# A four-layer hybrid decoder step on one core: the last S5 layer's parameter products are formed in the feed-forward before it and kept in DRAM

## The chip, the cores and the metric

The kernel runs on one core of a Trainium2 chip. The core has TensorE (matmul), VectorE, ScalarE and GpSimd, and a SyncE queue (SP) from which DMAs are issued. The metric is device time of one execution in microseconds; the median of several runs counts. The stretches of time below are microseconds from the start of the profiled span.

## The reference

One inference step of a four-layer trunk, for 512 prompt positions and 8 single-token samples that share all weights (width 1024, all in float32). Layer 0 and layer 3 have an S5 mixer, layer 1 stick-breaking attention, layer 2 a chunked gMLP; each mixer is followed by a SwiGLU feed-forward of width 2816, and every sub-layer stands between two RMS norms. The S5 mixer, shortened:

```python
u  = xn @ w_in                                   # 64 groups of 16 channels
ar, ai = mag * cos(li * dt), mag * sin(li * dt)  # one complex decay per group and state
bur = einsum('blgp,gnp->lbgn', ug, b_re)         # inputs to 64 states per group
...
hr, hi = scan(h[l] = a * h[l-1] + q * bu[l])     # complex, over the positions
y = einsum('lbgn,gpn->blgp', hr, c_re) - einsum('lbgn,gpn->blgp', hi, c_im) + d_skip * u
out = val * sigmoid(gate),  val, gate = split(gelu(y) @ w_glu)
```

The products that the change moves hold parameters alone: powers of the decay a times B (input matrix), C times powers of a (output matrix), and C a^k B (chunk matrix). None of them depends on x.

## The kernel before

Activations lie transposed: 8 tiles of 128 channels by 520 columns (512 positions, 8 samples), in two halves of 256 and 264. All weight products are done in three float32r matmuls (high times high, high times low, low times high; `mm`, L233 to L236). A weight tile of 128 output channels is loaded to `raw` (L194, two buffers), rounded to `wh` on ScalarE (L204) and its rest formed to `wl` on VectorE (L206). SP, ScalarE and VectorE do that some items ahead of TensorE.

A small planner writes the program. TensorE's work moves a model clock `self.t` on (`pe`); generators (`spawn`) run beside it and give, by `yield`, after how much model time, or on which condition, their next piece is put into the program. `until` runs the generators on till a condition holds. A scheduler then fixes each engine's order from that program with a timing model; on the chip each engine, and SP as a queue, works strictly in that order.

Between two sub-layers stands a *turn* (`turn`, L410 on): for each half the last output items end, the mean square is summed on TensorE, an inverse root made on VectorE and spread by a matmul (L365), then VectorE and ScalarE form the new x and its high and low parts (L421, L423, L405, L406), and the same sum, root and spread (a second L365) give the scale `rs` of the next sub-layer.

The S5 layer cuts 512 positions into 64 chunks of 8. `s5_begin` and `s5_prep` make the small tables (decays' powers `ap`, `b`, `c`); for the last layer that is done beside the gMLP. `s5_pipe` then goes over 8 tiles of 128 channels. Per tile it forms

- `powers_b` (L735 to L737): `ba` = B times powers, six products of 512 elements, on GpSimd (VectorE for tile 0), with `tn` as scratch;
- `powers_c` (L751, L761 to L763): `ca` = C times powers, half on VectorE, half on GpSimd, with `at` a copy of the powers and `tm` scratch;
- `blocks` and `kernels` (L743, L771, L776, L777): the chunk matrix from `ca` and `bd` on TensorE, written to DRAM as `dk` and read back shifted by eight DMAs as `wn` (L784);
- `inputs`: `rot` loaded (L789), `ba` transposed on TensorE (L797) and copied to `wi` (L800);
- `chunks`: the tile's `u` stored to DRAM and read back by chunk as `uq` (L805, L808);
- `scan`: matmuls with `wi` (L819), rotation, running scan and rotation back on VectorE (L827 to L843);
- `outputs` and `finish`: matmuls of `uq` with `wn` and `hm` with `ca` (L851, L852), transposes (L864), gelu.

The pipeline runs as a generator; `u` of the tiles comes from the layer's input matmuls, the first four in both halves first. When all eight outputs are there, the GLU follows. In the feed-forward (`ffn`) 22 hidden tiles are made in chunks of 6, 8 and 8 (`CHUNKS`), each followed by a pass over the 8 output tiles. In the feed-forward before the last S5 layer, TensorE has these matmuls and nothing else.

## Time and profile before

| | us |
|---|---|
| runs, median of 3 | 2790.7 (2788.12 to 2790.83) |
| the profiled execution's own time | 2778.86 |
| its span | 2777.1 |
| TensorE busy | 2552.3 (92%) |
| VectorE busy | 1592.4 (57%) |
| ScalarE busy | 1020.6 (37%) |
| GpSimd busy | 567.5 (20%) |

The span is read by stage: the feed-forward of layer 2 lies from about 1675 to 2080, the turn from it to the S5 layer from 2068 to 2131, the tile pipeline of the S5 layer from there to 2271, then GLU, and the last feed-forward. A stretch in which TensorE is busy throughout is limited by it; where it is not, the chain of waits and the other engines' busy time say by what.

### The profile page before, as it was taken

Reading aid. Unit: us, or ns where it says so; the run is one execution under the profiler, and the core shown is the slowest. Engines: PE = TensorE matmul, PEld = TensorE weight load, DVE = VectorE, ACT = ScalarE, POOL = GpSimd, SP = SyncE. Lnnn points to the kernel's source line nnn. Section 1 sums busy time; section 2 is a strip of 40 time slices with the busy share of each in tenths; the row PEclk is TensorE's granted clock in tenths of the full one; section 3 lists DMA queues with packets and bytes.
Section 4 is the critical chain, followed back from the end, with each engine's and each line's share of the span. In section 5 each row is a group of like instructions: output and inputs, shape, how many; then the busy total and the mean of one; then the engine's idle time right before and its main releaser. Section 6 shows DMA issues by size and latency. Waiting matters only on the chain.

```text
span 2777.1 us, 49812 instructions
## 1 busy us (share of the span) xinstructions
PE 2552.3 (92%) x20826; PEld 2442.3 (88%) x20826; DVE 1592.4 (57%) x2702; ACT 1020.6 (37%) x1697; POOL 567.5 (20%) x564
## 2 busy tenths in 40 slices
PE   7769999999897888999999899999997679999998
PEld 5659999999885557999999899999997569999998
DVE  8883643434659985734346777343458864634344
ACT  5443433222345464432223654322233433432221
POOL 5661300000337841200001203000004730200000
PEclk8879999999999999999999999999998889999998
DMA  4533233332245753233324231333322524233331
GB/s 116 144 94 93 69 92 107 92 92 77 97 125 177 225 160 100 69 99 92 92 77 96 84 113 58 106 99 92 92 73 50 138 51 130 59 102 92 92 92 45
DMA packets 476544, 274.49 MB, mean 99 GB/s; under 512 B 51912, under 2 KB 458720, under 8 KB 476320
## 3 DMA queue, kind: packets, MB, share of 16 engines
q1 hardware_dynamic: 467104, 237.76, 30.4%
q0 software_dynamic: 9216, 33.56, 3.6%
q8 instruction: 164, 2.69, 0.4%
q14 instruction: 60, 0.49, 0.1%
HBM read 253.60 MB, written 17.66 MB: 98 GB/s over the span
## 4 chain that ended last, share of the span: by engine, by line
PE 48%; DVE 11%; ACT 3%; DMA 2%; issue 2%; POOL 1%; SPq 0%; ACTq 0%; DVEq 0%; POOLq 0%
PE pp L233 15%; PE pp L234 15%; PE pp L236 15%; DVE wl L206 1%; DVE m L1241 1%; DMA raw<-in_w_ffn_in_dram 1%; ACT wh L204 1%; DVE pn L421 1%; DVE x L423 1%; DVE hm L843 1%; DMA raw<-in_w_cm_out_dram 1%; POOL x L423 0%; DVE xl L406 0%; PE psr L365 0%; DVE o L831 0%
## 5 line engine op out<-in xcount | busy, mean ns | idle before, releaser
L233 PE MATMUL pp<-xh,wh 128*128 128x264 f32 (+1 forms) x4480 | 1205.3, 287 | 25.5 <-ACT xh L405 4.7
L234 PE MATMUL pp<-xl,wh 128*128 128x264 f32 (+1 forms) x4480 | 1208.6, 286 | 7.1 <-DVE xl L406 7.0
L236 PE MATMUL pp<-xh,wl 128*128 128x264 f32 (+1 forms) x4480 | 991.4, 285 | 7.3 <-POOL wl L206 5.6
L233 PEld LDWEIGHTS pp<-xh,wh 128*128 128x128 f32 x4480 | 851.0, 190 | 36.3 <-issue 6.5
L234 PEld LDWEIGHTS pp<-xl,wh 128*128 128x128 f32 x4480 | 853.0, 190 | 11.4 <-DVE xl L406 9.9
L204 ACT ACTIVATE wh<-raw 128x1024 fp32r<-128x1024 f32 (+1 forms) x376 | 390.2, 1041 | 1126.5 <-PE pp L234 808.1
L236 PEld LDWEIGHTS pp<-xh,wl 128*128 128x128 f32 x4480 | 737.0, 190 | 12.0 <-POOL wl L206 5.8
L206 DVE TENSOR_TENSOR wl<-raw,wh 128x1024 fp32r<-128x1024 f32 (+1 forms) x356 | 439.1, 1236 | 322.0 <-ACT wh L204 310.8
L234 PE MATMUL pp<-hl,wh 128*128 128x256 f32 (+1 forms) x1408 | 377.2, 283 | 0.0
L233 PE MATMUL pp<-hh,wh 128*128 128x256 f32 (+1 forms) x1408 | 376.0, 283 | 0.0
L236 PE MATMUL pp<-hh,wl 128*128 128x256 f32 (+1 forms) x1408 | 314.4, 282 | 0.0
L234 PEld LDWEIGHTS pp<-hl,wh 128*128 128x128 f32 x1408 | 265.1, 188 | 0.0
L233 PEld LDWEIGHTS pp<-hh,wh 128*128 128x128 f32 x1408 | 264.9, 188 | 0.0
L236 PEld LDWEIGHTS pp<-hh,wl 128*128 128x128 f32 x1408 | 231.4, 188 | 0.0
L1579 DVE TENSOR_TENSOR tg<-pp,rs 128x520 f32<-128x520 f32 (+2 forms) x100 | 62.6, 632 | 231.9 <-PE pp L236 231.9
L1590 DVE TENSOR_TENSOR tg<-pp,tg 128x520 f32<-128x520 f32 (+2 forms) x96 | 62.6, 653 | 221.5 <-PE pp L236 221.2
L338 POOL TENSOR_TENSOR acc<-acc,s 128x256 f32<-128x256 f32 (+1 forms) x96 | 83.6, 870 | 450.2 <-ACT s L334 447.8
L1602 DVE TENSOR_TENSOR op<-pp,op 128x520 f32<-128x520 f32 (+2 forms) x88 | 48.4, 550 | 178.9 <-PE pp L236 178.8
L206 POOL TENSOR_TENSOR wl<-raw,wh 128x1024 fp32r<-128x1024 f32 x20 | 48.4, 2424 | 332.7 <-ACT wh L204 314.8
L405 ACT ACTIVATE xh<-x,gt 128x264 fp32r<-128x264 f32 (+1 forms) x128 | 62.9, 505 | 59.0 <-DVE x L423 45.1
L406 DVE SCALAR_TENSOR_TENSOR xl<-x,gt,xh 128x264 fp32r<-128x264 f32 (+1 forms) x128 | 78.7, 631 | 1.6 <-ACT xh L405 1.2
L642 POOL MEMSET ap<- 128x32 f32 x2 | 0.3, 175 | 359.0 <-PE pp L236 359.0
(334 smaller groups left out, 2890.7 us busy)
## 6 DMA issues: line engine op xcount, KB each, us to landing
raw<-in_w_ffn_in_dram SPq DMA_DIRECT2D x176, 512.0 KB
raw<-in_w_ffn_out_dram SPq DMA_DIRECT2D x64, 512.0 KB
raw<-in_w_ssm_glu_dram SPq DMA_DIRECT2D x32, 512.0 KB
raw<-in_w_ffn_out_dram SPq DMA_DIRECT2D x32, 384.0 KB
raw<-in_w_sb_qkv_dram SPq DMA_DIRECT2D x24, 512.0 KB
raw<-in_w_ssm_in_dram SPq DMA_DIRECT2D x16, 512.0 KB
wn<-dk SPq DMA_DIRECT2D x128, 64.0 KB
raw<-in_w_cm_in_dram SPq DMA_DIRECT2D x16, 512.0 KB
```

The costliest lines, as they stand in the source:

```text
L204: nc.scalar.activation(wh[:, :nk], raw[:, :nk], AF.Copy)
L206: on.tensor_tensor(wl[:, :nk], raw[:, :nk], wh[:, :nk], op=ALU.subtract)
L233: nc.tensor.matmul(ps(*h), lhsT=wh[:, k, :], rhs=xh[:, h[0]:h[1]], start=first, stop=False)
L234: nc.tensor.matmul(ps(*h), lhsT=wh[:, k, :], rhs=xl[:, h[0]:h[1]], start=False, stop=False)
L236: nc.tensor.matmul(ps(*h), lhsT=wl[:, k, :], rhs=xh[:, h[0]:h[1]], start=False, stop=last)
L338: i = (nc.gpsimd if pool else nc.vector).tensor_tensor(acc[0][:, c0:c1], acc[0][:, c0:c1], sq[:, :n], op=ALU.add)
L405: nc.scalar.activation(xs[k][0][:, c0:c1], self.x[k][:, c0:c1], AF.Copy, scale=g)
L406: return nc.vector.scalar_tensor_tensor(xs[k][1][:, c0:c1], self.x[k][:, c0:c1], g, xs[k][0][:, c0:c1], op0=ALU.mult, op1=ALU.subtract)
L421: nc.vector.scalar_tensor_tensor(t[:, :n], ops[k][:, c0:c1], self.gain(which_post, layer, k), ps[:, :n], op0=ALU.mult, op1=ALU.mult)
L1579: v.tensor_tensor(g, ps(c0, c1), rs[:, c0:c1], op=ALU.mult)
L1590: v.tensor_tensor(t, ps(c0, c1), t, op=ALU.mult)
L1602: v.tensor_tensor(o, ps(c0, c1), o, op=ALU.add)
```

## The change

A new generator `s5_stash` runs beside the feed-forward of layer 2. It forms, for each of the 8 tiles, `ba` and its transpose `wi`, `ca`, and the chunk matrix (with all element-wise products on VectorE), and stores them to DRAM tiles `wid`, `cad` and `wnd`, the chunk matrix already shifted, by eight stores. In `s5_pipe`, where these are there (`kept`), `powers_b`, `powers_c`, `kernels` and `blocks` are left out, and `inputs` loads `wi`, `ca` and `wn` instead; `wi` and `rot` get two buffers. The feed-forward with a stash works in chunks of 4, 6, 6, 6, with 7 instead of 9 buffers for hidden tiles, and waits before its last output items until the stash is issued. In all feed-forwards the silu is done in place, without the tile `sg`. Layer 0's S5 is not changed.

```diff
--- before.py
+++ after.py
@@ -27,6 +27,7 @@
 DFF = 2816
 FT = DFF // 128
 CHUNKS = (6, 8, 8)
+CHUNKS2 = (4, 6, 6, 6)
 EPS = 1e-6
 MAGIC = 12582912.0
 LA = 2
@@ -52,6 +53,7 @@
 WX = (4, 4, 2, 4)
 GMY = (12.0, 6.0, 14.0, 0.5)
 OLA, FLA = 4, 2
+STASH = (5.0, 3.0)
 TWO_PI_DOWN = 6.283185
 
 
@@ -710,11 +712,83 @@
         S["ok"] = True
         p.release()
 
+    def s5_stash(self, j):
+
+        nc, v = self.nc, self.nc.vector
+        S = self.S5[j]
+        p = self.tc.alloc_tile_pool(name="s5w", bufs=1, side="right")
+        wi_d = S["wi"] = [self.dr.tile([128, 2, 512], F32, name=f"wid{t}", bufs=1) for t in range(KT)]
+        ca_d = S["ca"] = [self.dr.tile([128, 8, 144], F32, name=f"cad{t}", bufs=1) for t in range(KT)]
+        wn_d = S["wn"] = [self.dr.tile([128, 8, 128], F32, name=f"wnd{t}", bufs=1) for t in range(KT)]
+        bd = p.tile([128, 4, 2, 2, 16], F32, name="bdw")
+        nc.gpsimd.memset(bd, 0.0)
+        B, ap, C = S["b"], S["ap"], S["c"]
+        for t in range(KT):
+            P = slice(4 * t, 4 * t + 4)
+            at = p.tile([128, 2, 4, 2, 9], F32, tag="at", name="atw")
+            for d in range(2):
+                for b in range(2):
+                    s = slice(64 * b, 64 * b + 64)
+                    nc.scalar.activation(at[64 * d:64 * d + 64, :, :, b, :], ap[s, :, P, :], AF.Copy)
+                    nc.scalar.activation(bd[64 * d:64 * d + 64, :, b, b, :], B[s, d, P, :], AF.Copy)
+            for ri in range(2):
+                ba = p.tile([128, 4, 8, 16], F32, tag="ba", name="baw")
+                m1 = p.tile([128, 576], F32, tag="m1", name="m1w")
+                m = m1[:, :512].rearrange("p (a r c) -> p a r c", a=4, r=8)
+                bb = [B[:, q, P].unsqueeze(2).to_broadcast([128, 4, 8, 16]) for q in (ri, 1 - ri)]
+                ab = [ap[:, q, P, 7::-1].unsqueeze(3).to_broadcast([128, 4, 8, 16]) for q in range(2)]
+                v.tensor_tensor(ba, bb[0], ab[0], op=ALU.mult)
+                v.tensor_tensor(m, bb[1], ab[1], op=ALU.mult)
+                v.tensor_tensor(ba, ba, m, op=ALU.subtract if ri == 0 else ALU.add)
+                yield STASH[0]
+                ps = self.bk.tile([128, 512], F32, tag="b", name="psw")
+                for a in range(4):
+                    nc.tensor.transpose(ps[:, 128 * a:128 * a + 128], ba[:, a].rearrange("p r c -> p (r c)"), self.ident)
+                self.t += 0.45
+                wi = p.tile([128, 512], F32, tag="wi", name="wiw")
+                nc.scalar.activation(wi, ps, AF.Copy)
+                nc.sync.dma_start(wi_d[t][:, ri], wi)
+                yield STASH[1]
+            ps = None
+            for hf in range(2):
+                G = slice(8 * t + 4 * hf, 8 * t + 4 * hf + 4)
+                sh = [128, 4, 9, 16]
+                ca = p.tile([128, 4, 9, 16], F32, tag="ca", name="caw")
+                m = p.tile([128, 576], F32, tag="m1", name="m1w").rearrange("p (g k c) -> p g k c", g=4, k=9)
+                cs = [C[:, q, G].unsqueeze(2).to_broadcast(sh) for q in range(2)]
+                ad = [at[:, q].rearrange("p a b k -> p (a b) k")[:, 4 * hf:4 * hf + 4].unsqueeze(3).to_broadcast(sh)
+                      for q in range(2)]
+                v.tensor_tensor(ca, cs[0], ad[0], op=ALU.mult)
+                v.tensor_tensor(m, cs[1], ad[1], op=ALU.mult)
+                v.tensor_tensor(ca, ca, m, op=ALU.subtract)
+                nc.sync.dma_start(ca_d[t][:, 4 * hf:4 * hf + 4], ca.rearrange("p g k c -> p g (k c)"))
+                yield STASH[0]
+                if ps is None:
+                    ps = self.bk.tile([128, 512], F32, tag="b", name="pskw")
+                for g in range(2):
+                    for a in (2 * hf, 2 * hf + 1):
+                        nc.tensor.matmul(ps[32 * a:32 * a + 32, :128], lhsT=bd[:, a, g].rearrange("p g c -> p (g c)"),
+                                         rhs=ca[:, 2 * a + g - 4 * hf, 0:8].rearrange("p k c -> p (k c)"),
+                                         start=g == 0, stop=g == 1, tile_position=(0, 32 * a))
+                self.t += 0.3
+                if hf == 0:
+                    yield STASH[1]
+            kp = self.kpad[t % 2]
+            nc.scalar.activation(kp[:, 144:], ps[:, 16:128], AF.Copy)
+            v.scalar_tensor_tensor(kp[:, 128:144], self.mod, self.gt[:, 128 + j * KT + t:129 + j * KT + t], ps[:, :16],
+                                   op0=ALU.mult, op1=ALU.add)
+            for r in range(8):
+                nc.sync.dma_start(wn_d[t][16 * r:16 * r + 16].rearrange("p g x -> g p x"),
+                                  kp[:, 128 - 16 * r:256 - 16 * r])
+            yield STASH[1]
+        p.release()
+
     def s5_pipe(self, S, us, ready, pools, rot, j, zs):
 
         nc, v, gp = self.nc, self.nc.vector, self.nc.gpsimd
         T = [{} for _ in range(KT)]
         pa = pools["a"] = self.tc.alloc_tile_pool(name="s5a", bufs=1)
+        kept = "wi" in S
 
         def sl(t):
             return slice(4 * t, 4 * t + 4)
@@ -784,13 +858,21 @@
                 nc.sync.dma_start(wn[16 * r:16 * r + 16], dv[:, :, 128 - 16 * r:256 - 16 * r])
 
         def inputs(t):
-            ba = T[t]["ba"]
-            rot_ = T[t]["rot"] = tp.tile([128, 4, 2, 64], F32, tag="rot", name="rot", bufs=1)
+            rot_ = T[t]["rot"] = tp.tile([128, 4, 2, 64], F32, tag="rot", name="rot", bufs=1 + kept)
             nc.sync.dma_start(rot_, rot[:, sl(t)])
             rho = T[t]["rho"] = tp.tile([128, 4, 64], F32, tag="rho", name="rho", bufs=1)
             nc.scalar.activation(rho, S["rho"][:, sl(t)].unsqueeze(2).to_broadcast([128, 4, 64]), AF.Copy)
             gp.memset(rho[:, :, 0:1], 0.0)
+            if kept:
+                wi = T[t]["wi"] = tp.tile([128, 2, 4, 128], F32, tag="wi", name="wi")
+                nc.sync.dma_start(wi.rearrange("p i a c -> p i (a c)"), S["wi"][t])
+                ca = T[t]["ca"] = pa.tile([128, 8, 9, 16], F32, tag="ca", name="ca", bufs=3)
+                nc.sync.dma_start(ca.rearrange("p g k c -> p g (k c)"), S["ca"][t])
+                wn = T[t]["wn"] = tp.tile([128, 8, 128], F32, tag="wn", name="wn")
+                nc.sync.dma_start(wn, S["wn"][t])
+                return
             pt, _ = self.pair()
+            ba = T[t]["ba"]
             for ri in range(2):
                 for a in range(4):
                     q = 4 * ri + a
@@ -872,8 +954,9 @@
         def stage(f, t):
             if 0 <= t < KT:
                 f(t)
-        powers_b(0)
-        powers_c(0)
+        if not kept:
+            powers_b(0)
+            powers_c(0)
         yield lambda: S["ok"]
         tp = pools["t"] = self.tc.alloc_tile_pool(name="s5t", bufs=2)
         S["uq"] = [tp.tile([128, 8, 80], F32, name=f"uq{q}", bufs=1) for q in range(3)]
@@ -887,9 +970,9 @@
         for q in [h[:, :, :, 8] for h in S["hm"]] + [S["bd"]]:
             gp.memset(q, 0.0)
         for t in range(-3, KT + 1):
-            if t > -2:
+            if t > -2 and not kept:
                 stage(powers_b, t + 2)
-            if t > -1:
+            if t > -1 and not kept:
                 stage(powers_c, t + 1)
             if 0 <= t + 1 < KT:
                 if t < 0:
@@ -897,8 +980,9 @@
                 stage(scan, t + 1)
                 yield S5Y[1]
             stage(finish, t - 1)
-            stage(kernels, t + 1)
-            stage(blocks, t + 2)
+            if not kept:
+                stage(kernels, t + 1)
+                stage(blocks, t + 2)
             yield S5Y[2]
             stage(inputs, t + 2)
             yield S5Y[3]
@@ -1563,7 +1647,10 @@
         w_in, w_out = self.w["ffn_in", l], self.w["ffn_out", l]
         xs, rs = st["xs"], st["rs"]
         wide = nxt is not None and nxt[1] % 3 != 0
-        with tc.tile_pool(name="hp", bufs=9) as hp, tc.tile_pool(name="ft", bufs=2) as ft, \
+        stash = nxt is not None and not wide
+        chunks = CHUNKS2 if stash else CHUNKS
+        keep = self.spawn(self.s5_stash(nxt[1] // 3)) if stash else None
+        with tc.tile_pool(name="hp", bufs=max(chunks) + 1) as hp, tc.tile_pool(name="ft", bufs=2) as ft, \
                 tc.tile_pool(name="wx", bufs=WX[2 + wide]) as wx:
             self.more_weights(wx, WX[2 + wide])
             ops = [None] * KT
@@ -1575,10 +1662,9 @@
                     if c0 == 0:
                         tg[m] = ft.tile([128, N], F32, tag="tg", name="tg", bufs=3)
                     g = tg[m][:, c0:c1]
-                    sg = ft.tile([128, N], F32, tag="sg", name="sg")[:, c0:c1]
                     v.tensor_tensor(g, ps(c0, c1), rs[:, c0:c1], op=ALU.mult)
-                    nc.scalar.activation(sg, g, AF.Silu)
-                    v.tensor_tensor(g, sg, rs[:, c0:c1], op=ALU.mult)
+                    nc.scalar.activation(g, g, AF.Silu)
+                    v.tensor_tensor(g, g, rs[:, c0:c1], op=ALU.mult)
                 return f
 
             def up_evict(m):
@@ -1600,12 +1686,12 @@
                     else:
                         o = ops[m][:, c0:c1]
                         v.tensor_tensor(o, ps(c0, c1), o, op=ALU.add)
-                        if c == len(CHUNKS) - 1:
+                        if c == len(chunks) - 1:
                             self.acc_square(acc, o, c0, c1, m == 0, m == KT - 1)
                 return f
 
             items, ends, m = [], [], 0
-            for c in CHUNKS:
+            for c in chunks:
                 for _ in range(c):
                     items += [(w_in, 0, m, gate_evict(m)), (w_in, 0, FT + m, up_evict(m))]
                     m += 1
@@ -1613,9 +1699,9 @@
             self.lead(items[:LEAD], st, nxt=items[LEAD:LEAD + 2])
             done = LEAD
             m0 = 0
-            for c, n in enumerate(CHUNKS):
+            for c, n in enumerate(chunks):
                 outs = [(w_out, m0, k, out_evict(k, c)) for k in range(KT)]
-                if c + 1 < len(CHUNKS):
+                if c + 1 < len(chunks):
                     e = ends[c] + 2
                     self.full(items[done:e], xs, KT, nxt=outs[:2], nnk=n)
                     done = e
@@ -1625,6 +1711,8 @@
                     hx = [hs[m0 + k] for k in range(n)]
                     k = KT - TAIL
                     self.full(outs[:k], hx, n, group=k, nxt=outs[k:], nnk=n, la=FLA, home=1 if wide else None)
+                    if keep is not None:
+                        self.until(lambda: keep["done"])
                     after, st = self.turns("ffn_post", l, ops, acc, nxt)
                     self.split(outs[k:], hx, n, after=after, nxt=self.first(nxt), early=wide, edge=0)
                 m0 += n
```

## Rows read from the trace of the kernel before

**Rows 1.** The page: busy us, share of the span, instructions, by engine

```profile
PE 2552.3 (92%) x20826; PEld 2442.3 (88%) x20826; DVE 1592.4 (57%) x2702; ACT 1020.6 (37%) x1697; POOL 567.5 (20%) x564
```

**Rows 2.** Stretches: length; busy us (count) PE, PEld, DVE, ACT, POOL; PEclk; DMA; GB/s

```profile
703.00:748.00 45.00, 43.07 (x351) 41.57 (x350) 37.04 (x107) 19.52 (x42) 19.27 (x28) 1.00 0.17 50
1675.00:1722.00 47.00, 43.63 (x358) 42.42 (x357) 34.22 (x97) 19.50 (x46) 19.57 (x21) 1.00 0.08 24
1722.00:2062.00 340.00, 340.00 (x2830) 339.82 (x2828) 139.75 (x172) 95.59 (x123) 2.40 (x1) 1.00 0.32 94
2068.00:2131.00 63.00, 46.67 (x314) 43.48 (x312) 56.63 (x118) 26.92 (x72) 27.51 (x34) 0.84 0.13 38
2147.00:2272.00 125.00, 84.33 (x838) 75.10 (x834) 105.92 (x153) 55.91 (x130) 77.94 (x73) 0.81 0.43 109
2256.00:2264.00 8.00, 6.33 (x68) 5.43 (x62) 7.38 (x15) 4.50 (x8) 1.27 (x2) 0.99 0.30 74
```

**Rows 3.** Chain of waits, last S5 layer: start us, length us, engine, tile, line

```profile
2146.69 1.18 PE pp L819 x32
...
2160.75 4.53 DMA raw<-in_w_ssm_glu_dram
...
2208.98 2.95 DMA rot<-rotd
...
2255.17 1.25 PE pp L819 x32
```

**Rows 4.** VectorE groups, 2147:2255: count, busy us, mean ns, idle before

```profile
L843 DVE TENSOR_TENSOR hm<-o 64x256 f32<-64x256 f32 x28 | 20.2, 722 | 0.6
...
L833 DVE TENSOR_TENSOR_SCAN o<-rho,o 128x256 f32<-128x256 f32 x14 | 11.9, 887 | 0.0
```

**Rows 5.** The same, last tile alone, 2256.4:2264.2

```profile
L843 DVE TENSOR_TENSOR hm<-o 64x256 f32<-64x256 f32 x4 | 2.2, 558 | 0.1
L833 DVE TENSOR_TENSOR_SCAN o<-rho,o 128x256 f32<-128x256 f32 x2 | 1.4, 686 | 0.0
```

**Rows 6.** TensorE's waits, 2147:2272: us in total, times, longest

```profile
PE psk L771 <- DVE ca L763: 24.7, 5, 7.3
```

**Rows 7.** VectorE groups in the turn, 2080:2110: count, busy us, mean ns

```profile
L762 DVE TENSOR_TENSOR tm<-cn,at 128x576 f32<-128x576 f32 x4 | 4.1, 1034 | 0.0
...
L761 DVE TENSOR_TENSOR ca<-cn,at 128x576 f32<-128x576 f32 x3 | 3.2, 1072 | 0.0
L763 DVE TENSOR_TENSOR ca<-ca,tm 128x576 f32<-128x576 f32 x3 | 3.1, 1036 | 0.0
L737 DVE TENSOR_TENSOR ba<-ba,tn 128x512 f32<-128x512 f32 x2 | 2.4, 1216 | 0.0
L736 DVE TENSOR_TENSOR tn<-bbar,ap 128x512 f32<-128x512 f32 x2 | 2.3, 1162 | 0.0
L735 DVE TENSOR_TENSOR ba<-bbar,ap 128x512 f32<-128x512 f32 x2 | 2.0, 994 | 0.0
```

**Rows 8.** Order of time, TensorE, ends of the turn: start us, length us

```profile
2068.52 0.61 PE L365 MATMUL psr<-ident,y 128*128 128x128 f32 x4
...
2131.48 0.92 PE L365 MATMUL psr<-ident,y 128*128 128x128 f32 x6
```

**Rows 9.** The page: DMA queues, packets, MB, share of 16 engines

```profile
q1 hardware_dynamic: 467104, 237.76, 30.4%
q0 software_dynamic: 9216, 33.56, 3.6%
```

**Rows 10.** Order of time, TensorE: kernel matmuls and transposes of one tile

```profile
2133.41 0.43 PE L771 MATMUL psk<-ca,bd 128*32 128x128 f32 x8 [0.43 <-ACT bd L743]
...
2137.11 1.03 PE L797 MATMUL pp<-ident,ba 128*128 128x128 f32 x8
```

## The prediction

> **What bounds the kernel now.** I read the share of busy time first: TensorE is busy in 92% of the span, VectorE in 57%, GpSimd in 20% [rows 1]. That average hides two different kinds of stage, so I then read busy time by stage [rows 2]. In the feed-forward of layer 2 (1722 to 2062 us) TensorE is busy in all 340 us at full clock, with VectorE at 41% and GpSimd at less than 1%: whatever is put on TensorE there is paid in full, and VectorE and ScalarE have room. In the last S5 layer (2147 to 2272) it is the other way round: VectorE is busy for 105.92 of 125 us, GpSimd for 77.94, TensorE for only 84 and with a granted clock of 0.81. And between them, in the turn from the feed-forward to the S5 layer (2068 to 2131), VectorE is busy for 56.63 of 63 us while TensorE falls to 46.67.
>
> The chain of waits and the order of time say what the S5 layer waits for. The first `scan` on TensorE starts at 2146.69, the eighth and last at 2255.17 [rows 3]: 108.48 / 7 = 15.5 us from tile to tile. One tile's own work on VectorE, seen alone in the last tile, when no products run beside it, is 15 instructions and 7.38 us (2256 to 2264, [rows 2]). The other 8.1 us of a period are the products of the parameters (`ba`, `tn`, `ca`, `tm`): half of `ca` on VectorE, the rest on GpSimd, and a slowing of VectorE while GpSimd works: the running scan (L833) takes 887 ns on average in these periods and 686 ns in the last tile, and `hm` (L843) 722 against 558 [rows 4, 5]. TensorE's longest wait in the stage says the same: the kernels (L771) wait 24.7 us in five waits for `ca` [rows 6].
>
> **The change, part by part.**
>
> *The turn.* Before, the first products fall into the turn, on the one engine that the turn needs: between 2080 and 2110 VectorE spends 4.1 + 3.2 + 3.1 + 2.4 + 2.3 + 2.0 = 17.1 us on them [rows 7]. The turn, from the first half's first broadcast on TensorE (L365) to the second half's last one, lasts from 2068.52 to 2131.48, 63.0 us [rows 8]; the same turn from the first feed-forward to attention, with no products in it, is the stretch from 703 to 748, 45 us [rows 2]. With `kept` none of these products is left. Forecast: 18.0 us off, bounds 14 to 18 (some copies and loads stay). Behind it the first half's matmuls and then rs come earlier by as much, so the first `scan` does too. The new loads for tiles 0 and 1 (about 3.3 MB with `ca`) fall into a stretch in which DMA is busy for 13% [rows 2], so they are hidden; without that cover they would cost one landing, some 5 us.
>
> *The period of the tile pipeline.* Removed per tile: six products on GpSimd and three half ones each on VectorE and GpSimd, eight transposes and sixteen kernel matmuls on TensorE, the copies for `bd`, `at`, `wi` and `kpad` on ScalarE, and on SP's queue one store and eight loads of 64 KB of `wn`. Added per tile on the same queue: `wi` (512 KB), `ca` (576 KB) and `wn` (512 KB), while `rot` gets a second buffer, so that VectorE's wait for it goes (landing 2.95 us, in the chain at 2208.98 [rows 3]). What is late next? Three floors. VectorE: the 7.4 us of the clean tile. DMA: a tile then moves 0.26 (`rot`) + 0.27 (`du`) + 0.30 (`uq`) + 0.52 + 0.59 + 0.52 = 2.46 MB; the SP queue's packets move 237.76 MB in 30.4% of 2777 us, 282 GB/s, and the queue with rows of some 3.6 KB 33.56 MB in 3.6%, 336 GB/s [rows 9]; so 7.3 to 8.7 us of all 16 engines. TensorE: 84 us for eight tiles in 2147 to 2272, the removed work and the last of the layer's input matmuls in it [rows 2], so at most 10.5 a tile, and less at full clock. These run beside each other, but they are close to each other, and loads wait: `wn` of tile t+2 takes the buffer that `outputs` of tile t still reads, and the eight `uq` loads of tile t+3, which wait for the same matmuls, stand behind it on SP. Landing of a 512 KB load takes 4.53 us in the chain [rows 3]; `wn` is needed two periods later, so it fits if the period is over about (4.5 + 4) / 2. I take 9.5 us, a tenth above the DMA's upper floor, bounds 7.4 and 13: 7 x (15.5 - 9.5) = 42 us off (a period of 7.4 would give 57, of 13 only 17.5). The S5 layer as a whole: 60 us off.
>
> The rates of VectorE here are where a rule can be weighed. The rows show its instructions longer beside GpSimd's, by 29% in the mean for both lines [rows 4, 5]. The Trainium skill, page "SBUF — State Buffer", section "Who interferes with whom", says that VectorE and GpSimd share a pair of ports that is held for a whole instruction, so that a VectorE instruction with two SBUF inputs blocks behind one of GpSimd that reads SBUF. By that rule the blocking in this stage ends altogether with GpSimd's products and the tile runs at VectorE's clean time; it is the third rival below.
>
> *The feed-forward of layer 2.* TensorE has no idle time there, so its added work is paid. Per tile eight transposes at 1.03 us (L797 x8) and twice eight kernel matmuls at 0.43 us (L771 x8) [rows 10]: 1.9 us, times 8 tiles 15 us. Each tile interrupts the stream of matmuls four times; the trace doesn't show that switch here, so between 0 and 0.2 us each, I take 0.06, 2 us for 32. Together 17, bounds 13 and 22. Each interruption is also a place where TensorE, in order, can wait for VectorE's products. They are issued a model time of 5 us ahead (`STASH`), and even at 1.07 us each (the mean of L761 in the crowded turn, [rows 7]) twelve products are 13 us in some 36 us, in which VectorE is idle for 59%, 21 us. I take 0.1 us each, 3 us, bounds 0 and 8.
>
> On ScalarE (95.59 of 340 busy) and VectorE (139.75) the copies and products are hidden [rows 2]; so are the fourth chunk's eight more evictions. Without that cover each would delay a PSUM eviction and then TensorE. On SP the weight loads queue behind stores that wait for ScalarE or VectorE; weights are loaded two items ahead, and DMA is 32% busy, so I count nothing, up to 5 us if the short four-tile chunk runs dry. The silu in place changes no count. The stash starts in the turn into this feed-forward (1675 to 1722), in which VectorE is busy for 34.22 of 47 us and TensorE for 43.63 [rows 2]: one tile's 8 to 13 us of products go there, of which 0 to 10 delay the chain; I take 4. The last step, waiting until the stash is done, costs nothing if all of it has been issued: eight tiles of about 36 model us are 289, and the feed-forward has about 320 before that point. Sum: 17 + 3 + 4 = 24 us more.
>
> **The sum.** 24 - 18 - 42 = -36 us. The profiled execution took 2778.86 us, with a span of 2777.1; it would take 2743. It lay 12 us under the median of the runs (2790.7), so the forecast is made as a difference to that median: 2755.
>
> **Rivals.**
>
> *The loads set the period.* A tile waits for SP's queue and for landings instead of products. For it: 1.1 MB more per tile, two tiles ahead at most, loads that already end in the chain (2.95 and 4.53 us, [rows 3]). Against it: SP issues fewer DMAs per tile, and DMA is at 43% in the stage. With 13 us: 18 + 17.5 - 24 = 12 us off, 2779.
>
> *Slower: TensorE waits in the feed-forward.* Its place is the 32 groups of transposes and kernel matmuls in the stream that has no idle time now. If each waits w for a product, 32w is added. In the S5 layer the same kernels wait 24.7 / 5 = 4.9 us each [rows 6]. Against it: VectorE is nearly full there and 59% idle here. The gain is eaten from w = 36 / 32 + 0.1 = 1.2 us; with 1.5 us the kernel takes 2790.7 - 36 + 45 = 2800.
>
> *The clean floor.* Blocking is gone and the loads hide: a period of 7.4 us gives 7 x 8.1 = 57 us there, 57 + 18 - 24 = 51 off, 2740. For it: the last tile shows it [rows 2]. Against it: the DMA floor of up to 8.7.
>
> *It doesn't do what it says.* If the stash is late, the rest of it is issued in one lump ahead of the last output items; the margin of 30 model us speaks against it, and it would still leave the S5 gain.
>
> **How the numbers follow.** Forecast 0.60 (its own range, with periods of 8 to 11.5 us and costs of 17 to 32 us, is 2738 to 2777), loads set the period 0.15, TensorE waits 0.10, clean floor 0.13, the rest 0.02. The range that should hold 8 in 10 reaches from a little under the clean floor's 2740 to a little over the loads' 2779: 2736 to 2784. Faster by over 0.2% (5.6 us, about what a measurement of this kernel can tell): all of the forecast and of the clean floor, most of the loads' case, 0.85; within it 0.06; slower 0.09.
>
> **What would show it.** In the profile after: the turn at about 45 us; the starts of L819's eight groups 9.5 us apart (7.4: the clean floor; 13 and up with DMA in the chain: the loads); no product of `ba` or `ca` on GpSimd from the last feed-forward's start on; the feed-forward of layer 2 at about 17 + 7 us more, with TensorE still without idle time; if the new kernel matmuls there head the table of waits, the second rival holds. I am wrong if the period falls but the layer doesn't get shorter, or if the feed-forward grows by over 32 us.

## The result, and the profile after

| | before | after |
|---|---|---|
| median of the runs, us | 2789.9 (2788.12 to 2790.83) | 2752.8 (2752.02 to 2755.05) |
| ratio, 95% interval | | 0.9885 (0.987 to 0.990) |
| the profiled execution's own time | 2778.86 | 2755.05 |
| its span | 2777.1 | 2752.9 |

Faster, by about 1.1%; the time lies 2 us under the predicted one. Executions of either kernel differ by up to 16 us in a stage that the change doesn't touch (attention lasts 347 to 363 us in the profiles of this case), so I read the change stage by stage from the two profiled executions. The stages are cut at the first and last spread of a norm on TensorE (the line that was L365 and is L367 after) and at the first matmul of the first and last `scan` (L901 after):

| stage, us | before | after | difference | forecast |
|---|---|---|---|---|
| up to the end of the turn into the gMLP | 1543.2 | 1545.3 | +2.1 | 0 |
| gMLP | 132.3 | 138.3 | +6.0 | 0 |
| turn into the feed-forward of layer 2 | 46.0 | 50.3 | +4.3 | +4 |
| that feed-forward | 347.0 | 375.3 | +28.3 | +20 |
| turn into the last S5 layer | 63.0 | 45.1 | -17.9 | -18 |
| from there to the first scan | 15.1 | 15.1 | 0 | 0 |
| first to last scan | 108.5 | 61.7 | -46.8 | -42 |
| the rest | 521.9 | 521.8 | -0.1 | 0 |
| span | 2777.1 | 2752.9 | -24.2 | -36 |

So the two traces differ by 24 us, where I forecast 36 and the medians differ by 37. A second series of the changed kernel on another chip (below) came out 24 us under before as well. So it is partly luck that the time lies within 2 us of the forecast: by the traces and by that series, I forecast half as much again as was gained.

The page's first section, busy us by engine, answers [rows 1]: GpSimd fell from 567.5 to 471.9 us, TensorE's sum stayed.

```profile
PE 2550.8 (93%) x20826; PEld 2444.0 (89%) x20826; DVE 1602.9 (58%) x2784; ACT 1023.0 (37%) x1713; POOL 471.9 (17%) x499
```

The stretches of after (length; busy us and count of PE, PEld, DVE, ACT, POOL; granted clock; DMA share; GB/s), in order the turn into the feed-forward, the feed-forward of layer 2, the turn into the S5 layer, the way to the first scan, and the tile pipeline from first to last scan, answer [rows 2]:

```profile
1683.60:1733.90 50.30, 46.80 (x375) 45.32 (x375) 42.20 (x108) 22.23 (x53) 20.13 (x21) 0.97 0.13 44
1733.90:2109.20 375.30, 372.96 (x3124) 367.52 (x3123) 210.00 (x300) 125.60 (x213) 2.37 (x1) 1.00 0.41 121
2109.20:2154.30 45.10, 34.38 (x241) 32.42 (x240) 33.42 (x95) 18.34 (x47) 16.17 (x24) 0.85 0.38 134
2154.30:2169.40 15.10, 15.10 (x125) 14.86 (x123) 9.49 (x22) 4.12 (x5) 0.00 (x0) 1.00 0.58 166
2169.40:2231.10 61.70, 48.43 (x532) 45.96 (x532) 50.97 (x110) 27.98 (x61) 1.83 (x13) 0.89 0.80 237
```

TensorE still has next to no idle time in the feed-forward (372.96 of 375.3), now with 3124 instead of 2887 instructions. The turn is 45.1 us. In the pipeline VectorE's 50.97 us and TensorE's 48.43 both leave room in 61.7, GpSimd has gone (1.83), and DMA is at 80%. For comparison the same stretch of before, first to last scan:

```profile
2146.60:2255.20 108.60, 70.54 (x709) 62.45 (x708) 97.67 (x137) 48.42 (x116) 71.22 (x64) 0.80 0.47 117
```

The first and the last scan in the order of time on TensorE, after ([rows 3] for before): 61.68 / 7 = 8.8 us a tile instead of 15.5.

```profile
2169.43 1.22 PE L901 MATMUL pp<-uq,wi 128*64 128x72 f32 x32
...
2231.11 1.22 PE L901 MATMUL pp<-uq,wi 128*64 128x72 f32 x32 [1.47 <-ACT ys L938]
```

The chain of waits in the pipeline of after (start us, length us, what) now passes through loads:

```profile
2193.62 4.06 DMA ca<-cad
...
2204.71 7.56 DMA wn<-wnd
...
2214.11 6.42 DMA wn<-wnd
2220.54 1.83 DMA uq<-du
```

TensorE's wait of 24.7 us for `ca` [rows 6] is gone; its longest in the pipeline (us in total, times, longest) is now for the reload of `u`:

```profile
PE pp L901 <- DMA uq<-du: 8.3, 3, 2.9
```

VectorE's groups there (count, busy us, mean ns, idle before) answer [rows 4, 5]: `hm` takes 420 ns instead of 722, the running scan 674 instead of 887.

```profile
L925 DVE TENSOR_TENSOR hm<-o 64x256 f32<-64x256 f32 x26 | 10.9, 420 | 0.7
L915 DVE TENSOR_TENSOR_SCAN o<-rho,o 128x256 f32<-128x256 f32 x14 | 8.9, 674 | 0.0
...
L913 DVE TENSOR_TENSOR o<-o,o 128x256 f32<-128x256 f32 x14 | 5.3, 420 | 0.2
L909 DVE TENSOR_TENSOR o<-pp,rot 128x512 f32<-128x512 f32 x7 | 4.8, 690 | 4.7 <-PE pp L901 2.4 <-DMA rot<-rotd 2.2
```

### The profile page after: what moved, and what is told of

Same layout as the page of the kernel before. It is cut to its first block, busy times and chain, and to the rows that moved or that the text cites. A ratio compares the mean times of both kernels' runs of the same rounds, so it can differ in the third digit from the quotient of the medians.

```text
span 2752.9 us, 49917 instructions
## 1 busy us (share of the span) xinstructions
PE 2550.8 (93%) x20826; PEld 2444.0 (89%) x20826; DVE 1602.9 (58%) x2784; ACT 1023.0 (37%) x1713; POOL 471.9 (17%) x499
## 4 chain that ended last, share of the span: by engine, by line
PE 68%; DVE 13%; ACT 6%; DMA 5%; issue 3%; POOL 2%; SPq 1%; ACTq 0%; POOLq 0%; DVEq 0%
PE pp L235 21%; PE pp L236 21%; PE pp L238 21%; DVE m L1325 2%; DVE wl L208 1%; DMA raw<-in_w_ffn_in_dram 1%; ACT wh L206 1%; DVE pn L423 1%; DVE x L425 1%; POOL kp L1189 1%; DMA rot<-rotd 1%; POOL x L425 1%; DVE o L915 1%; DMA raw<-in_w_sb_qkv_dram 1%; DVE xl L408 1%
## 5 line engine op out<-in xcount | busy, mean ns | idle before, releaser
L206 ACT ACTIVATE wh<-raw 128x1024 fp32r<-128x1024 f32 (+2 forms) x384 | 391.3, 1023 | 1090.2 <-PE pp L236 721.2
L208 DVE TENSOR_TENSOR wl<-raw,wh 128x1024 fp32r<-128x1024 f32 (+2 forms) x364 | 438.1, 1206 | 306.9 <-ACT wh L206 304.3
L1688 DVE TENSOR_TENSOR op<-pp,op 128x520 f32<-128x520 f32 (+2 forms) x96 | 54.0, 562 | 167.6 <-PE pp L238 167.4
L1325 DVE TENSOR_TENSOR_SCAN m<-m,e 128x512 f32<-128x512 f32 (+3 forms) x64 | 65.6, 1076 | 10.5 <-ACT e L1323 10.4
```

What stands on the lines that cost most here:

```text
L206: nc.scalar.activation(wh[:, :nk], raw[:, :nk], AF.Copy)
L208: on.tensor_tensor(wl[:, :nk], raw[:, :nk], wh[:, :nk], op=ALU.subtract)
L1325: v.tensor_tensor_scan(m[:, a:b][:, ::-1], m[:, a:b][:, ::-1], e[:, a:b][:, ::-1], 0.0, op0=ALU.add, op1=ALU.add)
```

## The experiments

Three questions: what set the pipeline's new period, what the feed-forward's 28 us are, and where the gMLP's 6 us come from. Series on other chips are compared with runs of before on the same chip: 2781.9, 2783.9 and 2781.4 us there.

**Repeats.** Before again, unchanged:

> The kernel before, unchanged, to see how far one execution's stages lie from another's. The profiled pair differs by 2777.1 - 2752.9 = 24 us while the medians differ by 37. My theory: the stages that the change touches repeat within 1 us (turn into the S5 layer 63.0, first to last scan 108.5, feed-forward of layer 2 346.9 us) and the 12 us lie in stages that it does not touch. The rival: the pipeline of the S5 layer itself varies by some us.

Measured 2780.4 us, ratio 0.9987 (0.9972 to 1.0002); profile: gMLP 134.5, feed-forward 347.0, turn into the S5 layer 63.4, first to last scan ("scans" from here on) 109.0. And the changed kernel again:

> The changed kernel, unchanged, on the same chip as the three below, for their comparison. If the stages that the change touches repeat: 61 to 63 us from the first to the last scan of the S5 layer, 45 for the turn, 375 for the feed-forward of layer 2, and 25 to 40 us under the kernel before.

Measured 2759.5 us, ratio 0.9911 (0.9895 to 0.9928); feed-forward 376.6, turn 46.5, scans 63.1, gMLP 139.0. The stages that the change touches repeat within 1.5 us; the gMLP of before does not (132.3 and 134.5).

**The chunks alone, in the kernel before.**

```diff
+CHUNKS2 = (4, 6, 6, 6)
-        with tc.tile_pool(name="hp", bufs=9) as hp
+        chunks = CHUNKS2 if nxt is not None and not wide else CHUNKS
+        with tc.tile_pool(name="hp", bufs=max(chunks) + 1) as hp
```

> The kernel before, with the feed-forward of layer 2 in chunks of 4, 6, 6, 6 and seven hidden buffers, and nothing else. After the change that feed-forward takes 375.3 us against 347.0, 28.4 more, where I forecast 20. My theory, that TensorE's added instructions and their switches are the cost: 347 to 349 here, the whole kernel within 0.1% of before. The rival, that short chunks make TensorE wait for weights: 352 us or more.

Measured 2793.5 us, ratio 1.0037 (1.0025 to 1.0049). My expectation fell: the feed-forward takes 355.5 us, 8.5 more. The rival had the size (352 or more) and not the reason, for TensorE is busy in all of the stretch, so nothing ran dry. The feed-forward and the turn behind it in this kernel:

```profile
1730.70:2086.20 355.50, 355.50 (x2956) 355.28 (x2955) 154.20 (x212) 103.89 (x139) 2.40 (x1) 1.00 0.33 94
2086.20:2150.70 64.50, 39.55 (x240) 36.24 (x239) 52.95 (x112) 23.46 (x67) 33.72 (x35) 0.76 0.10 29
```

The turn holds 240 TensorE instructions and 39.55 us; before it held 314 and 46.67 [rows 2]. The six output items that are kept back to cover the turn (`TAIL`) take three matmuls per hidden tile of the last chunk: 6 x 6 x 3 = 108 for a half instead of 6 x 8 x 3 = 144, so 72 fewer in both halves. The 74 that are missing are done in the feed-forward instead, where 69 more are counted: 74 x 0.12 us (355.5 us for 2956 of them) = 8.9 us.

This run has the changed kernel's chunks and products in their old place, so the step from it to the changed kernel is the stash without the chunks (and the silu in place): the feed-forward grows by 19.8 us (355.5 to 375.3) and the turn shrinks by 19.4 (64.5 to 45.1).

**The stash without its TensorE work** (no transposes and no kernel matmuls; the layer's chunk and input matrices are therefore not the right ones).

```diff
-                for a in range(4):
-                    nc.tensor.transpose(ps[:, 128 * a:128 * a + 128], ...)
-                nc.scalar.activation(wi, ps, AF.Copy)
+                nc.scalar.activation(wi, ba.rearrange("p a r c -> p (a r c)"), AF.Copy)
...
-                        nc.tensor.matmul(ps[32 * a:32 * a + 32, :128], lhsT=bd..., rhs=ca...)
+                ps = ca.rearrange("p g k c -> p (g k c)")
```

> The changed kernel without the stash's transposes and kernel matmuls; wi is copied from ba as it is and the chunk matrix from ca, so these two hold other numbers. All products, copies, stores and loads stay. My theory: the feed-forward of layer 2 falls from 375 to 353 to 357 us, since TensorE's instructions and the switches around them are some 18 to 20 of the 28 us; the S5 layer stays as it is (first to last scan 61.7). The rival, that stores on SP, products on VectorE or short chunks hold TensorE up: it stays above 365.

Measured 2764.1 us, ratio 0.9936 (0.9915 to 0.9957). The feed-forward fell from 375.3 to 360.5 us, 14.8, which is less than I expected (353 to 357 us) and close to the prediction's 15 for TensorE's instructions. It isn't their part alone, for products left this stage too: VectorE issues 226 instructions in it instead of 300. And the whole became slower than the changed kernel. The gMLP and the feed-forward here:

```profile
1541.20:1698.10 156.90, 132.85 (x1063) 129.94 (x1061) 132.76 (x295) 97.56 (x186) 20.84 (x25) 0.95 0.42 127
...
1756.80:2117.30 360.50, 356.26 (x2944) 356.05 (x2943) 163.54 (x226) 105.03 (x146) 2.60 (x1) 0.99 0.34 100
```

VectorE issues 295 instructions in the gMLP stage instead of 243 after and 238 before: nothing of TensorE holds the products back any more, so they run ahead into the gMLP (156.9 us) and the turn behind it (58.7), where the chain needs VectorE.

**Transposes back in the S5 layer** (the DRAM tile holds `ba`; 8 transposes and a copy per tile in `inputs`).

```diff
-                    nc.tensor.transpose(ps[:, 128 * a:128 * a + 128], ba[:, a]..., self.ident)
-                nc.sync.dma_start(wi_d[t][:, ri], wi)
+                nc.sync.dma_start(wi_d[t][:, ri], ba.rearrange("p a r c -> p (a r c)"))
```

> The changed kernel with the transposes moved back: the stash stores ba untransposed, the S5 layer loads ba in place of wi (the same bytes), transposes it on TensorE and copies it to wi (one buffer). My theory, that the period of the S5 layer is set by DMA and TensorE has idle time in it: the feed-forward of layer 2 falls by 9 to 11 us (16 groups of four transposes), the period stays at 8.8 to 9.2, and the kernel is 5 to 10 us under the changed one, about 2745. The rival, that TensorE and ScalarE are in the period's chain: it grows by 1 to 2 us in 7 periods and nothing is won.

Measured 2750.9 us, ratio 0.9888 (0.9869 to 0.9907). The feed-forward fell only 4.4 us, to 370.9, where I expected 9 to 11; the scans took 65.0 instead of 61.7, the touched stages together 3 us less. No difference that the runs can tell.

**The same with chunks of 4, 4, 7, 7** (and 8 buffers).

```diff
-CHUNKS2 = (4, 6, 6, 6)
+CHUNKS2 = (4, 4, 7, 7)
```

> The changed kernel with B times powers (not transposed) in the DRAM tiles and the transposes back in the S5 layer, as in the run with late transposes, and the feed-forward before it in chunks of 4, 4, 7, 7 instead of 4, 6, 6, 6, with 8 buffers for hidden tiles. Theory that the chunks cost 8.5 us because the last chunk's 6 hidden tiles leave less TensorE work for the turn: with 7 of them 18 matmuls per half are added to what covers the turn, so the feed-forward of layer 2 falls from 370.9 to 366 to 369 us and the turn stays at 45 to 47; the whole is 2 to 5 us faster than with late transposes alone, ratio 0.986 to 0.988. Rival, that the fourth chunk by itself costs the 8.5 us: 370 to 372.

Measured 2743.5 us, ratio 0.9863 (0.9833 to 0.9894): the lowest median of all, though the interval overlaps the changed kernel's (0.987 to 0.990). In the traces its touched stages together take 10 us less than the changed kernel's, with scans of 67.3 us. Feed-forward and turn, first with late transposes and chunks 4, 6, 6, 6, then with 4, 4, 7, 7:

```profile
1724.90:2095.90 371.00, 367.73 (x3065) 362.65 (x3064) 207.19 (x296) 117.34 (x194) 2.74 (x1) 0.99 0.41 120
2095.90:2141.60 45.70, 34.65 (x241) 32.69 (x240) 33.75 (x96) 18.37 (x47) 16.17 (x24) 0.85 0.37 132
```

```profile
1731.80:2099.20 367.40, 364.12 (x3042) 359.04 (x3041) 206.68 (x296) 117.23 (x194) 2.74 (x1) 1.00 0.41 121
2099.20:2137.90 38.70, 34.25 (x267) 31.73 (x266) 31.22 (x96) 17.61 (x47) 11.97 (x23) 1.00 0.38 134
```

The feed-forward lost 3.6 us and 23 instructions, the turn gained 26 (36 by the count). The tail theory holds, and the rival, that the fourth chunk by itself costs the 8.5 us, fell. But the turn got 7.0 us shorter instead of staying, with the clock at 1.00 instead of 0.85, which I had not expected. The order of time at its end shows why; first the changed kernel (GpSimd, VectorE, TensorE), then this one:

```profile
2139.76 4.64 POOL L208 TENSOR_TENSOR wl<-raw,wh 128x1024 fp32r<-128x1024 f32 x2 [2.23 <-ACT wh L206]
...
2140.76 1.37 DVE L379 TENSOR_SCALAR ii<-v 128x3 int32<-128x3 int32 x1
2142.17 2.26 DVE L380 TENSOR_SCALAR y<-ii 128x3 int32<-128x3 int32 x1
2144.35 1.89 DVE L1008 TENSOR_TENSOR u<-pp,rs 128x256 f32<-128x256 f32 x4
...
2145.94 0.56 PE L235 MATMUL pp<-xh,wh 128*128 128x264 f32 x1 [5.46 <-DVE u L1008]
```

```profile
2137.30 4.72 POOL L208 TENSOR_TENSOR wl<-raw,wh 128x1024 fp32r<-128x1024 f32 x2 [8.77 <-ACT wh L206]
...
2134.88 0.17 DVE L379 TENSOR_SCALAR ii<-v 128x3 int32<-128x3 int32 x1
2135.08 0.17 DVE L380 TENSOR_SCALAR y<-ii 128x3 int32<-128x3 int32 x1
```

In the changed kernel two `wl` of 2.3 us each stand on GpSimd from 2139.76, and the two VectorE instructions on three elements (L379, L380), 0.17 us each in the other kernel, take 1.37 and 2.26 us. TensorE waits 5.46 us for the `u` behind them, and its clock falls (3 us slices of the changed kernel; columns as in the stretches above):

```profile
2139.20:2142.20 3.00, 1.28 (x15) 1.16 (x14) 1.62 (x4) 1.70 (x3) 2.44 (x2) 0.83 0.03 5
2142.20:2145.20 3.00, 0.00 (x0) 0.00 (x0) 3.00 (x3) 0.00 (x0) 2.21 (x1) 0.50 0.56 164
2145.20:2148.20 3.00, 2.26 (x10) 2.29 (x11) 2.33 (x12) 0.00 (x0) 0.00 (x0) 0.50 0.63 185
2148.20:2151.20 3.00, 3.00 (x16) 3.00 (x15) 0.00 (x0) 0.00 (x0) 0.00 (x0) 0.50 0.00 0
```

In the last kernel the same `wl` starts at 2137.30, when the norm's small instructions are over. By an estimate from these rows, about 3.3 us of the 7 are the lengthening itself, and of the rest the half clock over the 6 us from 2145 to 2151 costs about 3. It is no more than an estimate: the two kernels' orders differ elsewhere in the turn too, and the last one has 26 more instructions to cover it. A kernel in which that `wl` alone is moved wasn't tried.

The same collision, with 1.36 to 1.38 and 2.26 to 2.27 us, stands in seven other traces with the stash and in that of the chunks alone, but in neither of before, where these instructions take 0.17 us. So it came with the cut to 4, 6, 6, 6 and not with the stash.

**GpSimd's products beside the pipeline** (results unused; the loops are shortened here).

```diff
                 nc.sync.dma_start(wn, S["wn"][t])
+                for _ in range(6): gp.tensor_tensor(tn[:, :512], <b>, <ap>, op=ALU.mult)
+                for _ in range(3): gp.tensor_tensor(tn, <c>, <ap>, op=ALU.mult)
                 return
```

> The changed kernel, and per tile of the last S5 layer nine element-wise products on GpSimd again (six of 512 and three of 576 elements, as before the change), whose results nobody reads. Theory that GpSimd's work beside the pipeline slowed VectorE: in the kernel before, GpSimd's products took 71 us of the 108.5 from first to last scan and VectorE's running scan was 887 instead of 686 ns, hm 722 instead of 558; so with them back VectorE's running scan goes from 640 to over 800 ns, VectorE's work per tile from 7.4 to about 9.5 us, the period from 8.8 to 10 to 12 us, first to last scan from 62 to 70 to 84. Rival, that the gain came from the waits for products alone: VectorE is busy for 51 of 62 us and has room, so the period stays at 8.8 to 9.2 (62 to 64 us), whatever the single instructions do.

Measured 2772.7 us, ratio 0.9977 (0.9957 to 0.9997), against 0.9885 and 0.9911 for the changed kernel: 18 to 26 us slower than that, so most of the net gain is gone. Turn and pipeline:

```profile
2093.80:2145.20 51.40, 38.84 (x240) 35.85 (x238) 45.88 (x95) 18.68 (x47) 40.96 (x47) 0.80 0.34 117
2161.30:2234.70 73.40, 52.01 (x533) 48.56 (x533) 69.30 (x101) 26.33 (x56) 47.95 (x52) 0.84 0.71 209
```

The period is 73.4 / 7 = 10.5 us, the turn 6.3 us longer. VectorE's groups in the pipeline:

```profile
L935 DVE TENSOR_TENSOR hm<-o 64x256 f32<-64x256 f32 x24 | 17.6, 732 | 0.6
L923 DVE TENSOR_TENSOR o<-o,o 128x256 f32<-128x256 f32 x14 | 14.1, 1045 | 0.2
L925 DVE TENSOR_TENSOR_SCAN o<-rho,o 128x256 f32<-128x256 f32 x13 | 10.1, 812 | 0.0
...
L919 DVE TENSOR_TENSOR o<-pp,rot 128x512 f32<-128x512 f32 x7 | 4.8, 690 | 2.2 <-PE pp L911 2.0
```

The instructions with both operands in SBUF grew (`hm` 420 to 732 ns, `o<-o,o` 420 to 1045, the running scan 674 to 812); the rotation out of PSUM did not (690 and 690). The rival fell: it counted on VectorE's 11 us of room, but the blocking added 18.3 us to VectorE's busy time (50.97 to 69.30), which is now 94% of the stretch.

**Only tiles 0 and 1 kept.**

```diff
-        for t in range(KT):
+        for t in [q for q in range(KT) if q < 2]:
...
-            if kept:
+            if kept(t):
```

> The changed kernel with only tiles 0 and 1 of the S5 layer formed in the feed-forward; tiles 2 to 7 form their products in the pipeline as before (rot and wi with one buffer). The turn into the S5 layer should be 45 to 48 us as after the whole change, the periods of tiles 2 to 7 should be back at 15 to 16 us (first to last scan 90 to 105), and the feed-forward of layer 2 should be 347 + 8.5 (chunks) + 15 / 4 (TensorE's work of two tiles) + 1 to 4 = 360 to 364. By my sum the whole takes 2765 to 2775 against some 2783 before. A rival, that the gain of the turn is given back by the pipeline, which then waits longer for its first products, would show periods over 17 us and a time no shorter than before.

Measured 2789.7 us, ratio 1.0036 (1.0012 to 1.006): my time was wrong, the rival's right, though its periods of over 17 us came only twice in seven. Turn and pipeline:

```profile
2086.10:2139.20 53.10, 36.71 (x240) 33.37 (x239) 43.79 (x100) 21.43 (x59) 30.77 (x35) 0.84 0.26 89
2154.40:2263.40 109.00, 73.41 (x670) 65.27 (x669) 92.17 (x132) 44.44 (x108) 62.42 (x57) 0.75 0.40 102
```

The turn was 53.1, not 45 to 48, because the products of tile 2 now fall into it (GpSimd is busy for 30.77 us instead of 16.17, VectorE for 43.79 instead of 33.42). The scans take 109.0 us though two tiles came ready: periods of 9.7, 13.9, 14.0, then 19.6, 12.7, 25.8 and 13.5. The feed-forward, at 359.7, cost 12.7. So with two tiles moved, the turn gains 9.9 us, less than the feed-forward costs, and the pipeline gains nothing. Numbers of tiles between two and eight weren't tried.

**What sets the period of 8.8 us.** First the `wi` loads doubled:

```diff
+                w2 = tp.tile([128, 2, 512], F32, tag="w2", name="w2", bufs=1)
+                nc.sync.dma_start(w2, S["wi"][t])
```

> The changed kernel with one more load of wi per tile (512 KB, into a tile that nobody reads). My theory, that DMA sets the period now (0.80 busy over the pipeline): 512 KB at some 330 GB/s of the 16 engines are 1.6 us more per tile, the first to the last scan takes 70 to 74 us instead of 61.7. The rival, that VectorE's 7.4 us set it: 62 to 64.

Measured 2754.6 us, ratio 0.9905 (0.9889 to 0.9922), scans 62.6 us. This tells nothing: nobody reads `w2`, so all second loads were issued before the pipeline, whose traffic stayed as it was. Then the eight `uq` loads put on ScalarE's queue instead of SP's:

```diff
-                nc.sync.dma_start(S["uq"][t % 3][16 * r:16 * r + 16, :, c0:c1],
+                (nc.scalar if kept else nc.sync).dma_start(S["uq"][t % 3][16 * r:16 * r + 16, :, c0:c1],
```

> The changed kernel with the eight uq loads of a tile issued from ScalarE's queue instead of SP's. Nothing is moved less. If DMA's engines are the pace: first to last scan stays at 60 to 63 us. The rival, that SP's queue is the pace, where the eight uq loads take some 6.4 us of 8.8 and the next tile's loads stand behind them: it falls to 54 to 57 us, and the kernel with it by 5 to 8 us.

Measured 2754.6 us, ratio 0.989 (0.9867 to 0.9913), scans 63.4 us: neither the time nor the scans fell. This doesn't clear SP's queue, though. On ScalarE the eight issues, 0.44 us each, and the waits in front of them stand between ScalarE's own instructions, and the `uq` loads are now 60.0% of the chain of waits in this stretch. Last, `ca` and `wn` loaded for tile 0 alone (code shortened):

```diff
-                ca = ... ; nc.sync.dma_start(ca, S["ca"][t]) ; wn = ... ; nc.sync.dma_start(wn, S["wn"][t])
+                if t == 0: (the same)
+                else: T[t]["ca"], T[t]["wn"] = T[0]["ca"], T[0]["wn"]
```

> The changed kernel, where the tiles of ca and wn are loaded for tile 0 alone and all eight tiles use tile 0's (so the layer's outputs are those of wrong matrices); 1.1 of 2.5 MB per tile less. Theory that the loads set the period of 8.8 us: without them the next floor is VectorE's clean 7.4 us, so 7 periods of 7.3 to 7.9, first to last scan 51 to 55 us. Rival, that the way of one tile through store, reload, matmuls, VectorE and PSUM sets it: 8.5 to 9 us as now, 60 to 64.

Measured 2745.6 us, ratio 0.9877 (0.9843 to 0.9911). The pipeline:

```profile
2163.10:2217.60 54.50, 47.28 (x534) 44.39 (x533) 47.54 (x102) 26.30 (x58) 1.71 (x12) 0.91 0.66 180
```

First to last scan 54.5 us, 7.8 a tile, in the range of the theory (51 to 55): the loads do set the period. By which of their costs stays open. In the changed kernel DMA's engines are busy for 0.80 of 8.8 us, 7.0 us a tile, so they are not full; but from 2203 us on SP is always either issuing a load or waiting for a landing before the next one, up to 2.5 us at a time (7.8 us in five waits for `wn` over the whole pipeline). This run took out the bytes and those waits together. What is under the loads isn't shown either: VectorE is busy for 47.54 us here, 6.8 a tile, and TensorE for 47.28.

**The gMLP.** The stash's pool opened inside the feed-forward, behind the gMLP:

```diff
-        p = self.tc.alloc_tile_pool(name="s5w", bufs=1, side="right")
+        p = self.tc.alloc_tile_pool(name="s5w", bufs=1)
...
-        keep = self.spawn(self.s5_stash(nxt[1] // 3)) if stash else None
...
             self.more_weights(wx, WX[2 + wide])
+            keep = self.spawn(self.s5_stash(nxt[1] // 3)) if stash else None
```

> The changed kernel with the stash's pool laid over memory that the gMLP's tiles hold until they are done, and its first step behind the feed-forward's pools; the work is the same. In the changed kernel seven of the stash's VectorE instructions run in the gMLP stage, from 1600 us on, and others in the turn into the feed-forward. My theory: these delay the gMLP (138.3 against 132.4 and 134.5 us) and the turn (50.3 against 46.0 and 47.4); here the two fall to 133 to 135 and 46 to 48, the feed-forward stays at 375 to 378, and the kernel is 3 to 7 us under the changed one. The rival, that they ran in idle time and the gMLP's length is chance: no change.

Measured 2755.2 us, ratio 0.9884 (0.9855 to 0.9914); gMLP 137.0 us. It did not do what I meant: the stash's first five VectorE instructions still stand in the gMLP, from 1612.8 us on (they are five in the changed kernel too, not seven). So whether they cost its 4 to 6 us stays open; that early products can cost much there is seen in the run without TensorE's work (156.9 us). The kernel with two tiles kept has a gMLP of 133.6 us with the same 243 VectorE instructions, five such among them, which speaks against these. In the eight traces with these five the stage takes 133.6 to 139.0 us, in the three without a stash 132.3 to 134.5. The gMLP of before, and of after (one row of each, columns as above):

```profile
1543.20:1675.50 132.30, 121.36 (x988) 118.64 (x987) 98.52 (x238) 76.53 (x121) 17.75 (x23) 0.97 0.36 105
```

```profile
1545.30:1683.60 138.30, 124.56 (x989) 121.73 (x988) 103.51 (x243) 78.33 (x129) 16.88 (x24) 0.95 0.35 101
```

## Why the prediction was right, point by point

- *The pipeline's period*: 8.8 us against my 9.5 (bounds 7.4 and 13). The reason I gave, a floor of DMA of 7.3 to 8.7 with a little on top, is borne out as far as it says that the loads set it: without 1.1 of 2.46 MB a tile the period falls to 7.8. That the engines of DMA are the floor isn't shown; they are busy for 7.0 us a tile, and SP's queue, which I took to be relieved by fewer issues, is full from 2203 us on. The first rival (13 us) had the right resource and the wrong size, with landings of 4.06 to 7.56 us in the chain. The clean floor, third rival, fell by 1.4 us a tile: the blocking did end, with every running scan at 0.66 to 0.68 us, but the loads came next.
- *The slowing by GpSimd*: it is real and worth 1.7 of the 6.7 us a tile (10.5 with unread products against 8.8); the other 5 are, by difference, the products on VectorE and the waits for them, which no run takes out alone. The rule of the Trainium skill that I weighed ("SBUF — State Buffer", "Who interferes with whom") agrees with the traces in its finer points too: the rotation, with one operand in PSUM, kept its 690 ns beside GpSimd. What I read as 29% in the mean is a few instructions blocked whole: of the running scans of before, eleven took 0.66 to 0.69 us and three 1.48 to 1.89. My clean tile was not quite clean either: two GpSimd products of the layer's final state start at 2262.73 us beside its last `hm`, so its 558 ns is a mean with a blocked one in it; alone `hm` takes 420.
- *The turn into the S5 layer*: -17.9 against -18.0, with two errors in it that nearly cancel. Taking the products out is worth 19.4 (64.5 to 45.1 with the same chunks); the cut of the chunks costs 1.5 (63.0 to 64.5), for which I counted nothing: with the cut come less cover for the turn and the collision of the two `wl` with the norm. I took 45 us from the other turn as a floor, and it was none: the version without the collision, and with a last chunk of 7, takes 38.7.
- *The feed-forward*: 28.3 against 20, the step that was mis-sized. The stash itself costs 19.8 (355.5 to 375.3): TensorE's busy time grows by 17.5 (355.50 to 372.96; forecast 17 with the switches), and 2.3 us are idle (forecast 3). But the chunks, for which I counted nothing and up to 5, cost 8.5. I looked for a weight load running dry; there was none. What I missed is the tail: the output items that cover the next turn shrink with the last chunk.
- *TensorE waits for products* (second rival): fell. TensorE's only wait in the feed-forward that the table lists is one of 2.3 us for an eviction; none stands before a kernel matmul or a transpose of the stash.
- *The turn into the feed-forward*: 4.3 against 4.
- *The gMLP*, +6.0 (134.5 and 139.0 in the repeats): not foreseen. I put the stash's start into the turn; its first products run already in the gMLP. Cause open: the same 243 VectorE instructions took 133.6 us in one run and 138.3 in another.
- *It doesn't do what it says*: fell; the stash's last store is issued at 2028, 81 us before the feed-forward's end.

The sum: better by 4.8 in the pipeline, worse by 8.3 in the feed-forward, 6.0 in the gMLP, 2.1 ahead of it, and the small rest, which gives the -24.2 of the traces.

## What to carry to other kernels

Parameter work that fills an engine in a latency-bound stage is worth moving to a TensorE-bound one even where TensorE pays for it, if enough of it is moved: with two of eight tiles the gain was nothing. Where a loop is cut anew to make room, count the matmuls that the cut takes from the tail that covers the next turn; the last chunk's size cost 8.5 us here, and chunks of 4, 4, 7, 7 with late transposes gave 2743.5 us, the lowest median found, if not clearly apart from the changed kernel. And keep long GpSimd instructions with SBUF operands away from the short VectorE instructions of a norm.

## What the runs showed of the hardware

- Beside two GpSimd products of 2.3 us each, two VectorE instructions on three elements lasted 1.37 and 2.26 us instead of 0.17. The Trainium skill, page "SBUF — State Buffer", section "Who interferes with whom", says that an instruction of this kind (tensor_scalar) can enter a mode that uses the pair of ports shared with GpSimd, and that whichever engine issues first keeps the pair for its whole instruction; the two instructions end at 2142.13 and 2144.43, about where the two `wl` end, which agrees. That they ran in that mode is not shown by itself.
- TensorE's granted clock fell to 0.50, the lower of its two levels (1.2 GHz), in a slice in which it had nothing to do (2142.2 to 2145.2), and stayed there for the next two slices, in which it was busy for 2.26 and 3.00 of 3 us. In the version with the shorter turn it stayed at 1.00 in every slice.
